# A seven-product QKV projection: row pairs 6 to 29 taken two at a time, all bf16 products of both first, then the float32r ones

## The chip, the cores and the metric

The kernel runs on one core of one Trainium2 chip. The metric is the device time of one execution in microseconds (us), as the median of several runs. The engines are named as the profile names them: PE (TensorE, matmuls), PEld (TensorE's weight loads), DVE (VectorE), ACT (ScalarE), POOL (GpSimd) and SP (SyncE, which here only issues DMAs).

## The reference

```python
# x: (16, 512, 768) float32, w_qkv: (768, 2304) float32
qkv = np.matmul(x, w_qkv)
q, k, v = qkv[..., :768], qkv[..., 768:1536], qkv[..., 1536:]
return np.stack([q, k, v], axis=0).astype(np.float32)
```

So 8192 rows of 768 are multiplied by a 768 x 2304 matrix, and the 2304 columns are stored as three outputs.

## The kernel before

**Tiling.** The 8192 rows are 32 *pairs* p of 2 x 128 rows. The 2304 columns are two *quads* q of 1024 columns each (0 to 1023, 1280 to 2303) and a *remainder* of 256 columns between them. Within a pair and a quad the product is a 2 x 2 block product: two row blocks of 128, two halves of the inner 768 (384 each, `KH` = 3 steps of 128), two column blocks of 512. It is done with seven block products instead of eight, from sums of the blocks of x and sums of the blocks of w. Each block product is three matmuls of 128 x 128 by 128 x 512 (`product`, L244). Products 1 and 2 use bf16 copies of x (`xb`) and w (`b1`). Products 3 to 7 use float32r sums of x (`s`, from `sums_x`) and of w (`t`, and the block `b22`). The remainder is a plain product in bf16: twelve matmuls of 256 columns per pair (`rem_row`, L299).

**A quad's work** is in `do(u, n)`. Three PSUM banks are used: x holds product 1 and then, added up in place, 6, 7 and 4; z holds product 2; y holds 5 and then 3. Each intermediate value of bank x is copied out by ACT (L253 after product 1, L269 after 6, L275 after 7, L279 after 4) into the output tile `o`, before the next product is added to the bank. DVE adds bank z to the first copy (L266), bank y to the copy after 7 (L276), and bank y again, once product 3 is in it, to the copy after 6 (L282). The eight PSUM banks come from one pool, and a new bank is one that its last reader has freed.

**A pair's x** goes through four steps. `load_x` brings it from HBM in four DMAs of 192 KB to `xin` (three buffers). `transpose` turns it on DVE (L154) into `xf` (two buffers). `round_x` casts it to bf16 on POOL (L191) into `xb` (four buffers). `sums_x` makes five float32r blocks on POOL (L211 to L215) in `s` (two buffers).

**Order.** The order is written by hand: the program order of each engine is the order of the calls. For pairs 3 to 30, `two(a, b, early)` issues for quads a and b of one pair: product 1 of both, the next pair's transpose, cast and sums (`ahead(p + 1)`) and the load of pair p + 2, the remainder, product 2 of both, then the ten float32r products 6, 6, 5, 7, 5, 7, 4, 3, 4, 3, with `store_quad` after each quad's product 3. A store of a quad is one DMA of 768 KB and one of 256 KB on SP's queue. Of a pair's four loads, two are issued on SP and two on ACT from pair 7 on. Pairs 0 to 2 are a start-up stage of their own, in which the weights are loaded, cast and summed; `last` does pair 31. The output tiles `o` have five buffers. One more tile, `both` (one buffer), serves the start-up and then holds one quad of pair 2.

Of the kernel before, what the change touches and what calls it, by code (L numbers as in the profile page):

```python
# [10 lines left out]
def kernel(  # L11
# [20 lines left out]
    nc = tc.nc  # L32
    P = 128
    G = 32
# [7 lines left out]
    NP = M // (2 * P)  # L42
# [18 lines left out]
    bt_pool = ctx.enter_context(tc.tile_pool(name="bt", bufs=1))  # L61
# [22 lines left out]
    both = bt_pool.tile([P, 2, KH * CB], fp32, name="both", tag="both")  # L84
# [37 lines left out]
    xin, xf, xb, sr = {}, {}, {}, {}  # L122
# [3 lines left out]
    def load_x_half(p, h, eng):  # L126
        rows = x_flat[p * 2 * P:(p + 1) * 2 * P, :].rearrange("(g b) k -> b g k", b=G)
        for i in (2 * h, 2 * h + 1):
            eng.dma_start(xin[p][i * G:(i + 1) * G], rows[:, :, i * KC:(i + 1) * KC])
# [12 lines left out]
    def load_x(p, other):  # L142
        xin[p] = xin_pool.tile([P, 2 * P // G, KC], fp32, name="xin")
        load_x_half(p, 0, nc.sync)
        if other is not None:
            load_x_half(p, 1, other)

    def transpose(p, parts=1):
        t = xf_pool.tile([P, KT, 2 * P], fp32, name="xf")
        turned = t[:].rearrange("p j (g b) -> p g j b", b=G)  # L150
        rows = xin.pop(p)[:].rearrange("p g (a j) -> p g j a", a=G)
        n = 2 * P // G // parts
        for g in range(0, 2 * P // G, n):
            nc.vector.transpose(turned[:, g:g + n], rows[:, g:g + n])  # L154
        xf[p] = t

# [27 lines left out]
            [xb[p][:, n, r * P:(r + 1) * P] for n in ks], [t[:] for t in ps]  # L186
        )

    def round_x(p):
        xb[p] = xb_pool.tile([P, KT, 2 * P], bf16, name="xb", tag="xb")  # L190
        nc.gpsimd.tensor_copy(out=xb[p][:], in_=xf[p][:])  # L191

    act, dve = nc.scalar, nc.vector

# [9 lines left out]
    def sums_x(p, eng=None):  # L204
        t = xf.pop(p)
        a11, a12 = t[:, :KH, :P], t[:, KH:, :P]
        a21, a22 = t[:, :KH, P:], t[:, KH:, P:]
        s = s_pool.tile([P, 5, KH, P], f32r, name="s")
        sr[p] = s
        sums = {  # L210
            1: lambda g: g.tensor_tensor(s[:, 1], a21, a22, op=add),  # L211
            2: lambda g: g.tensor_tensor(s[:, 2], s[:, 1], a11, op=sub),  # L212
            3: lambda g: g.tensor_tensor(s[:, 3], a11, a21, op=sub),  # L213
            0: lambda g: g.tensor_copy(out=s[:, 0], in_=a22),
            4: lambda g: g.tensor_tensor(s[:, 4], a12, s[:, 2], op=sub),  # L215
        }
        if eng is not None:
            return sums
        for n in (1, 2, 3, 0, 4):
            sums[n](nc.gpsimd)  # L220
# [5 lines left out]
    def quad(p, q, pool=o_pool, tag="o"):  # L226
        u = Quad()
        u.p, u.q = p, q
        u.o = pool.tile([P, 2, 2 * CB], fp32, name="o", tag=tag)
        u.x = u.y = u.z = None  # L230
        return u

    def product(u, n, ps, start):
        t1, t2, t3, t4 = ts[u.q]
        if n <= 2:
            h = (n - 1) * KH
            lhs = [xb[u.p][:, h + j, :P] for j in range(KH)]
            rhs = [b1[u.q][:, h + j, :] for j in range(KH)]
        else:
            k, t = {3: (4, b22[u.q][:]), 4: (0, t4), 5: (1, t1), 6: (2, t2), 7: (3, t3)}[n]  # L240
            lhs = [sr[u.p][:, k, j, :] for j in range(KH)]
            rhs = [t[:, j, :] for j in range(KH)]
        for j in range(KH):
            nc.tensor.matmul(  # L244
                ps[:], lhs[j], rhs[j],
                start=(start and j == 0), stop=(j == KH - 1), skip_group_check=True,
            )

    def bank():
        return ps_pool.tile([P, CB], fp32, name="ps")  # L250

    def evacuate(u):
        nc.scalar.activation(u.o[:, 0, :CB], u.x[:], ident)  # L253

    def do(u, n, out=True):
        c11, c12 = u.o[:, 0, :CB], u.o[:, 0, CB:]
        c21, c22 = u.o[:, 1, :CB], u.o[:, 1, CB:]
        if n == 1:
            u.x = bank()
            product(u, 1, u.x, True)  # L260
            if out:
                evacuate(u)
        elif n == 2:
            u.z = bank()
            product(u, 2, u.z, True)
            nc.vector.tensor_tensor(c11, c11, u.z[:], op=add)  # L266
        elif n == 6:
            product(u, 6, u.x, False)
            nc.scalar.activation(c12, u.x[:], ident)  # L269
        elif n == 5:  # L270
            u.y = bank()
            product(u, 5, u.y, True)
        elif n == 7:
            product(u, 7, u.x, False)
            nc.scalar.activation(c22, u.x[:], ident)  # L275
            nc.vector.tensor_tensor(c22, c22, u.y[:], op=add)  # L276
        elif n == 4:
            product(u, 4, u.x, False)
            nc.scalar.activation(c21, u.x[:], ident)  # L279
        elif n == 3:  # L280
            product(u, 3, u.y, False)
            nc.vector.tensor_tensor(c12, c12, u.y[:], op=add)  # L282
# [14 lines left out]
    def rem_row(p, r, ps):  # L297
        for j in range(KT):
            nc.tensor.matmul(  # L299
                ps, xb[p][:, j, r * P:(r + 1) * P], w_rem[j // KH][:, j % KH, :],  # L300
                start=(j == 0), stop=(j == KT - 1), skip_group_check=True,
            )

    def rem(p, eng=nc.sync, between=None):
        ps = ps_pool.tile([P, 2, REM], fp32, name="ps")
        rem_row(p, 0, ps[:, 0, :])
        if between is not None:
            between()
        rem_row(p, 1, ps[:, 1, :])
        return rem_copied(p, ps, eng)  # L310

    def rem_copied(p, ps, eng=nc.sync):

        def copied():
            o = or_pool.tile([P, 2, REM], fp32, name="orem")
            act.activation(o[:], ps[:], ident)  # L316
            return lambda: eng.dma_start(rows_of(1, p, R_OFF - H, R_OFF - H + REM), o[:])

        return copied
# [11 lines left out]
                        )  # L331
        return [rem_copied(p, ps) for p, ps in zip(pairs, banks)]

    def two(a, b, early, u=None):

        do(a, 1)
        do(b, 1, u is None)
        if u is None:
            early()
            rem(a.p)()()  # L340
        else:
            middle(u)
            copied = rem(a.p, between=lambda: third(u))
            evacuate(b)
            early()
            copied()()
            fourth(u)
        do(a, 2)
        do(b, 2)
        do(a, 6)  # L350
        do(b, 6)
        do(a, 5)
        do(a, 7)
        do(b, 5)
        do(b, 7)
        do(a, 4)
        do(a, 3)
        store_quad(a)
        do(b, 4)
        do(b, 3)  # L360
        store_quad(b)
# [14 lines left out]
    def last(a, b):  # L376

        p = a.p

        def rem_stored(r):  # L380
            ps = bank()
            rem_row(p, r, ps[:, :REM])
            o = or_pool.tile([P, 2, REM], fp32, name="orem")
            nc.scalar.activation(o[:, 0, :], ps[:, :REM], ident)  # L384
            row = (2 * p + r) * P
            nc.scalar.dma_start(out_flat[1, row:row + P, R_OFF - H:R_OFF - H + REM], o[:, 0, :])

        do(a, 1)
        do(b, 1)
        do(a, 2)  # L390
        do(a, 6)
        do(b, 2)
        do(b, 6)
        for u in (a, b):
            store_cols(u, 0, 0, CB, nc.sync)
        for u in (a, b):
            do(u, 5)
            do(u, 7)
            store_cols(u, 1, CB, 2 * CB, nc.sync)
        do(a, 4)  # L400
        store_cols(a, 1, 0, CB, nc.scalar)
        rem_stored(0)
        do(b, 4)
        store_cols(b, 1, 0, CB, nc.scalar)
        for u in (a, b):
            do(u, 3)
            store_cols(u, 0, CB, 2 * CB, nc.sync)
        rem_stored(1)


    ND = 2
# [21 lines left out]
    for h in range(2):  # L433
        rows = w_qkv.rearrange("(p j) n -> p j n", j=KT)[:, h * KH:(h + 1) * KH]
# [17 lines left out]
    quads = {}  # L452
# [45 lines left out]
    def fourth(u):  # L498
        do(u, 4)
        store_quad(u)  # L500

    def ahead(p):
        transpose(p)
        round_x(p)
        sums_x(p)
# [7 lines left out]
    turned = [turn_row(0, 0)]  # L513
# [49 lines left out]
    sums = sums_x(2, dve)  # L563
# [7 lines left out]
    u = quad(2, 0)  # L571
# [42 lines left out]
    u2 = quad(2, 1, bt_pool, "both")  # L614
    do(u2, 1)
    do(u2, 2)

    for p in range(ND + 1, NP):
        def early():
            if p + 1 < NP:  # L620
                ahead(p + 1)
            if p + 2 < NP:
                load_x(p + 2, nc.sync if p <= ND + 2 else nc.scalar)

        a, b = quad(p, 0), quad(p, 1)
        if p == ND + 1:
            two(a, b, early, u2)
        elif p < NP - 1:
            two(a, b, early)
        else:  # L630
            last(a, b)


# [28 lines left out]
```

## Time and profile before

| What | Value |
|---|---|
| Time, median of 3 runs | 360.9 us (360.07 to 361.46) |
| The profiled execution's own time | 360.84 us |
| Its span, first to last instruction | 359.1 us |
| Granted clock of TensorE, mean | 0.999 of full speed |
| PE busy | 353.6 us, 98% of the span |
| PEld, DVE, ACT, POOL busy | 70%, 64%, 52%, 50% |
| DMA: bytes, mean rate | 107.73 MB, 300 GB/s |

A group line of the profile gives the kernel's line, engine, operation, out<-in by the program's names, shapes, the count, then the busy time and the mean length in ns, and last the idle time of the engine ahead of these instructions with what ended it. Matmuls are pipelined, and their ends are modelled: the time that a matmul costs is the distance between starts, not its length. In the chain of waits and in a timeline, the first number is the start in us from the start of the span and the second is the length.

### The profile page before, as it was taken

What the parts mean: (1) busy time and instruction counts of PE and PEld (TensorE: products, weight loads), DVE (VectorE), ACT (ScalarE), POOL (GpSimd) and SP (SyncE); (2) the same over time, 40 slices, a digit from 0 to 9 for tenths busy, and PEclk for the clock granted to TensorE, in tenths of its full rate; (3) what the DMA queues carried; (4) which work ended last, traced back from release to release, by engine and by line L of the source; (5) the groups of instructions that cost most, each with busy time, mean ns of one, the idle gap of its engine ahead of it and who ended that gap; (6) DMA issues with size and microseconds to landing.
All of it is one profiled execution on the core that took longest, in us unless ns stands there. A gap on an engine that the chain in (4) does not pass through costs nothing.

```text
span 359.1 us, 5279 instructions
## 1 busy us (share of the span) xinstructions
PE 353.6 (98%) x1780; PEld 251.4 (70%) x1780; DVE 228.8 (64%) x244; ACT 185.7 (52%) x316; POOL 179.8 (50%) x187
## 2 busy tenths in 40 slices
PE   8999999999999999999999999999999999999995
PEld 3465577777777777777777777777777777777764
DVE  3789776666566675556676556676556676556643
ACT  5479644445444445444445444445544445545443
POOL 0223766446665445665444665444665444666420
PEclk9999999999999999999999999999999999999999
DMA  7998999898999998999999999898999899989767
GB/s 270 344 373 306 330 354 397 249 347 297 282 307 309 294 288 260 309 298 314 293 291 277 291 293 324 286 289 278 295 285 331 284 297 271 297 279 324 289 241 257
DMA packets 82106, 107.73 MB, mean 300 GB/s; under 512 B 5408, under 2 KB 62240, under 8 KB 82080
## 3 DMA queue, kind: packets, MB, share of 16 engines
q1 hardware_dynamic: 66672, 96.35, 82.1%
q10 hardware_dynamic: 14608, 10.65, 9.0%
q0 software_dynamic: 800, 0.39, 0.8%
q8 instruction: 14, 0.23, 0.3%
q14 instruction: 12, 0.10, 0.1%
HBM read 32.28 MB, written 75.50 MB: 300 GB/s over the span
## 4 chain that ended last, share of the span: by engine, by line
PE 92%; DMA 4%; ACT 2%; ACTq 1%; issue 0%
PE ps L244 78%; PE ps L299 10%; PE ps L472 4%; DMA st<-in_w_qkv_dram 3%; DMA touch<-in_x_dram 1%; PE ps L327 1%; ACT o L279 0%; ACTq L370 0%; ACT orem L316 0%; ACT o L462 0%; ACT orem L384 0%; ACT xb L200 0%; ACT both L448 0%; ACT o L253 0%; ACTq L416 0%
## 5 line engine op out<-in xcount | busy, mean ns | idle before, releaser
L244 PE MATMUL ps<-t,s 128*128 128x512 f32 x720 | 181.2, 399 | 0.1
L244 PEld LDWEIGHTS ps<-t,s 128*128 128x128 f32 x720 | 135.0, 188 | 31.1 <-ACT o L253 0.4
L191 POOL CAST xb<-xf 128x1536 bf16<-128x1536 f32 x28 | 40.9, 1462 | 131.4 <-DVE xf L154 131.4
L276 DVE TENSOR_TENSOR o<-o,ps 128x512 f32<-128x512 f32 x58 | 39.9, 688 | 90.7 <-ACT o L275 90.7
L154 DVE STREAM_TRANSPOSE xf<-xin 128x1536 f32<-128x1536 f32 (+1 forms) x32 | 88.9, 2782 | 2.3 <-DMA xin<-in_x_dram 2.3
L244 PE MATMUL ps<-b,xb 128*128 128x512 bf16 x360 | 87.7, 380 | 0.0
L244 PEld LDWEIGHTS <-xb 128*128 128x128 bf16 x360 | 32.8, 98 | 37.3 <-issue 7.6
L269 ACT ACTIVATE o<-ps 128x512 f32<-128x512 f32 x60 | 35.9, 598 | 43.8 <-PE ps L244 41.1
L275 ACT ACTIVATE o<-ps 128x512 f32<-128x512 f32 x58 | 34.7, 598 | 44.3 <-PE ps L244 44.3
L282 DVE TENSOR_TENSOR o<-o,ps 128x512 f32<-128x512 f32 x60 | 41.3, 688 | 21.4 <-PE ps L244 20.2
L244 PE MATMUL ps<-b,s 128*128 128x512 f32 x180 | 50.4, 389 | 0.0
L279 ACT ACTIVATE o<-ps 128x512 f32<-128x512 f32 x60 | 35.9, 598 | 24.5 <-PE ps L244 21.6
L253 ACT ACTIVATE o<-ps 128x512 f32<-128x512 f32 x60 | 35.8, 597 | 24.4 <-DVE o L282 20.6
L299 PE MATMUL ps<-w_rem,xb 128*128 128x256 bf16 x360 | 44.6, 273 | 0.0
L299 PEld LDWEIGHTS <-xb 128*128 128x128 bf16 x360 | 34.9, 98 | 11.1 <-issue 0.8
L266 DVE TENSOR_TENSOR o<-o,ps 128x512 f32<-128x512 f32 x60 | 37.8, 672 | 2.0 <-ACT o L253 1.3
L244 PEld LDWEIGHTS ps<-b,s 128*128 128x128 f32 x180 | 33.8, 188 | 7.1
L211 POOL TENSOR_TENSOR s<-xf 128x384 fp32r<-128x384 f32 x29 | 30.8, 1063 | 0.0
L212 POOL TENSOR_TENSOR s<-s,xf 128x384 fp32r<-128x384 f32 x29 | 29.4, 1013 | 2.3
L215 POOL TENSOR_TENSOR s<-xf,s 128x384 fp32r<-128x384 f32 x29 | 29.6, 1019 | 0.0
L213 POOL TENSOR_TENSOR s<-xf 128x384 fp32r<-128x384 f32 x29 | 29.4, 1015 | 0.0
L316 ACT ACTIVATE orem<-ps 128x512 f32<-128x512 f32 x31 | 18.5, 597 | 20.4 <-PE ps L299 19.9
(47 smaller groups left out, 127.0 us busy)
## 6 DMA issues: line engine op xcount, KB each, us to landing
out_dram<-o SPq DMA_DIRECT2D x62, 768.0 KB, 5.6
out_dram<-o SPq DMA_DIRECT2D x65, 256.0 KB, 4.2
xin<-in_x_dram SPq DMA_DIRECT2D x62, 192.0 KB, 6.9
xin<-in_x_dram ACTq DMA_DIRECT2D x50, 192.0 KB, 4.3
out_dram<-orem SPq DMA_DIRECT2D x31, 256.0 KB, 5.9
st<-in_w_qkv_dram SPq DMA_DIRECT2D x11, 256.0 KB, 5.1
st<-in_w_qkv_dram SPq DMA_DIRECT2D x3, 768.0 KB, 10.1
xin<-in_x_dram SPq DMA_DIRECT2D x4, 384.0 KB, 4.5
```

Of the source, the lines that this page charges most:

```text
L154: nc.vector.transpose(turned[:, g:g + n], rows[:, g:g + n])
L191: nc.gpsimd.tensor_copy(out=xb[p][:], in_=xf[p][:])
L211: 1: lambda g: g.tensor_tensor(s[:, 1], a21, a22, op=add),
L244: nc.tensor.matmul(ps[:], lhs[j], rhs[j], start=(start and j == 0), stop=(j == KH - 1), skip_group_check=True,)
L253: nc.scalar.activation(u.o[:, 0, :CB], u.x[:], ident)
L266: nc.vector.tensor_tensor(c11, c11, u.z[:], op=add)
L269: nc.scalar.activation(c12, u.x[:], ident)
L275: nc.scalar.activation(c22, u.x[:], ident)
L276: nc.vector.tensor_tensor(c22, c22, u.y[:], op=add)
L279: nc.scalar.activation(c21, u.x[:], ident)
L282: nc.vector.tensor_tensor(c12, c12, u.y[:], op=add)
L299: nc.tensor.matmul(ps, xb[p][:, j, r * P:(r + 1) * P], w_rem[j // KH][:, j % KH, :], start=(j == 0), stop=(j == KT - 1), skip_group_check= ...
```

## The change

Pairs 6 to 29 are done in groups of two by a new function `group(p)`. In a group PE does the bf16 work of both pairs (products 1 and 2 of the four quads, and both remainders), and then the float32r products of the first pair and of the second (`rounded`, split off from `two`). The first quad of a group takes the tile `both`.

POOL's order in a group is: the first sum of pair p + 1, the cast of pair p + 1, its other four sums, the cast of pair p + 2, and, once the first pair's float32r products are done, the sums of pair p + 2. DVE transposes pair p + 2 at the start of the group and pair p + 3 after the four product-2 adds.

Loads of x are all issued on SP: pairs p + 4 and p + 5 within the group. Before, pair p issues the load of pair p + 2; now pair 3 issues those of pairs 5 and 6, pair 4 that of pair 7, and pair 5 those of pairs 8 and 9. Pair 7's transpose is done in two halves within pair 5's float32r products. Pairs 30 and 31 are done singly, by `two` and `last`.

```diff
--- before.py
+++ after.py
@@ -145,14 +145,20 @@
         if other is not None:
             load_x_half(p, 1, other)
 
-    def transpose(p, parts=1):
+    def transpose(p, parts=1, split=False):
         t = xf_pool.tile([P, KT, 2 * P], fp32, name="xf")
         turned = t[:].rearrange("p j (g b) -> p g j b", b=G)
         rows = xin.pop(p)[:].rearrange("p g (a j) -> p g j a", a=G)
         n = 2 * P // G // parts
-        for g in range(0, 2 * P // G, n):
-            nc.vector.transpose(turned[:, g:g + n], rows[:, g:g + n])
+        turns = [
+            lambda g=g: nc.vector.transpose(turned[:, g:g + n], rows[:, g:g + n])
+            for g in range(0, 2 * P // G, n)
+        ]
         xf[p] = t
+        if split:
+            return turns
+        for turn in turns:
+            turn()
 
 
 
@@ -186,9 +192,10 @@
             [xb[p][:, n, r * P:(r + 1) * P] for n in ks], [t[:] for t in ps]
         )
 
-    def round_x(p):
+    def round_x(p, t=None):
+        t = xf[p] if t is None else t
         xb[p] = xb_pool.tile([P, KT, 2 * P], bf16, name="xb", tag="xb")
-        nc.gpsimd.tensor_copy(out=xb[p][:], in_=xf[p][:])
+        nc.gpsimd.tensor_copy(out=xb[p][:], in_=t[:])
 
     act, dve = nc.scalar, nc.vector
 
@@ -331,7 +338,7 @@
                         )
         return [rem_copied(p, ps) for p, ps in zip(pairs, banks)]
 
-    def two(a, b, early, u=None):
+    def two(a, b, early, u=None, turns=()):
 
         do(a, 1)
         do(b, 1, u is None)
@@ -347,12 +354,20 @@
             fourth(u)
         do(a, 2)
         do(b, 2)
+        rounded(a, b, turns)
+
+    def rounded(a, b, turns=()):
+
+        for t in turns[:1]:
+            t()
         do(a, 6)
         do(b, 6)
         do(a, 5)
         do(a, 7)
         do(b, 5)
         do(b, 7)
+        for t in turns[1:]:
+            t()
         do(a, 4)
         do(a, 3)
         store_quad(a)
@@ -615,20 +630,55 @@
     do(u2, 1)
     do(u2, 2)
 
-    for p in range(ND + 1, NP):
+    def group(p):
+
+        quads = [quad(p, 0, bt_pool, "both"), quad(p, 1)]
+        do(quads[0], 1)
+        do(quads[1], 1)
+        turned = xf[p + 1]
+        sums = sums_x(p + 1, nc.gpsimd)
+        sums[1](nc.gpsimd)
+        round_x(p + 1, turned)
+        for n in (2, 3, 0, 4):
+            sums[n](nc.gpsimd)
+        transpose(p + 2)
+        round_x(p + 2)
+        if p + 4 < NP:
+            load_x(p + 4, nc.sync)
+        rem(p)()()
+        do(quads[0], 2)
+        do(quads[1], 2)
+        quads += [quad(p + 1, q) for q in range(2)]
+        do(quads[2], 1)
+        do(quads[3], 1)
+        if p + 5 < NP:
+            load_x(p + 5, nc.sync)
+        rem(p + 1)()()
+        do(quads[2], 2)
+        do(quads[3], 2)
+        if p + 2 < NE:
+            transpose(p + 3)
+        rounded(*quads[:2])
+        sums_x(p + 2)
+        rounded(*quads[2:])
+
+    NG, NE = ND + 4, NP - 2
+    extra = {NG - 3: (NG, ), NG - 1: (NG + 3, )}
+    for p in range(ND + 1, NG):
+        late_turns = []
+
         def early():
-            if p + 1 < NP:
-                ahead(p + 1)
-            if p + 2 < NP:
-                load_x(p + 2, nc.sync if p <= ND + 2 else nc.scalar)
-
-        a, b = quad(p, 0), quad(p, 1)
-        if p == ND + 1:
-            two(a, b, early, u2)
-        elif p < NP - 1:
-            two(a, b, early)
-        else:
-            last(a, b)
+            ahead(p + 1)
+            for n in (p + 2 + (p > NG - 3), ) + extra.get(p, ()):
+                load_x(n, nc.sync)
+            if p == NG - 1:
+                late_turns.extend(transpose(NG + 1, 2, True))
+
+        two(quad(p, 0), quad(p, 1), early, u2 if p == ND + 1 else None, late_turns)
+    for p in range(NG, NE, 2):
+        group(p)
+    two(quad(NE, 0), quad(NE, 1), lambda: ahead(NE + 1))
+    last(quad(NE + 1, 0), quad(NE + 1, 1))
 
 
 # ---- launch: one core; inputs and outputs as the reference has them ----
```

## Prediction

> **What bounds the kernel now.** I read the page first (busy shares, groups), then the chain of waits in order of time, then TensorE's own timeline over one pair.
>
> ```profile
> span 359.1 us, 5279 instructions
> PE 353.6 (98%) x1780; PEld 251.4 (70%) x1780; DVE 228.8 (64%) x244; ACT 185.7 (52%) x316; POOL 179.8 (50%) x187
> PE 92%; DMA 4%; ACT 2%; ACTq 1%; issue 0%
> ```
>
> TensorE (PE) is on the chain for 92% of the span. The chain in order of time shows that from pair 4 on it never leaves PE:
>
> ```profile
> 195.39 1.31 PE ps L299 x12
> 196.70 9.43 PE ps L244 x42
> 206.13 1.31 PE ps L299 x12
> ```
>
> One pair is 206.13 - 195.39 = 10.74 us. An edit of the order can gain only by closing PE's own seams, and lose only by making PE wait. The seams are in PE's timeline (start, length, tile, count; ends are modelled, so starts are what to subtract):
>
> ```profile
> 181.14 0.84 PE L244 MATMUL ps<-b,s 128*128 128x512 f32 x3
> ...
> 183.18 1.47 PE L244 MATMUL ps<-b,xb 128*128 128x512 bf16 x6
> 184.49 1.47 PE L299 MATMUL ps<-w_rem,xb 128*128 128x256 bf16 x12
> 185.80 1.46 PE L244 MATMUL ps<-b,xb 128*128 128x512 bf16 x6
> 186.91 5.14 PE L244 MATMUL ps<-t,s 128*128 128x512 f32 x21
> 191.88 0.84 PE L244 MATMUL ps<-b,s 128*128 128x512 f32 x3
> ```
>
> Nine float32r products run from 181.14 to 183.18: 0.2267 us each. The twelve 256-wide ones take 1.31 us, 0.109 each. The sixth bf16 product of the last group is recorded at 186.88, so five steps take 1.08 us, 0.216 each. A pair without seams would be 30 x 0.2267 + 12 x 0.216 + 12 x 0.109 = 10.70 us. The seams cost 10.74 - 10.70 = 0.04 us per pair: about 0.015 where float32r gives way to bf16 (1.31 us for six, not 1.296), the rest at the start of the float32r run (21 products from 186.88 + 0.216 to 191.88 take 4.78 us, not 4.76). In that stretch GpSimd is casting:
>
> ```profile
> 187.00 1.46 POOL L191 CAST xb<-xf 128x1536 bf16<-128x1536 f32 x1 [4.78 <-DVE xf L154]
> ```
>
> **The change, part by part.**
>
> *Seams.* Pairs 6 to 29 are 24 pairs with 24 bf16 stretches now and 12 after. 12 x 0.04 = 0.48 us gained.
>
> *Casts out of the float32r run.* Each remaining seam loses its cast neighbour. The excess inside the float32r start is 0.02 us, so this is worth 0 to 0.02 us; I take 0.01 because the same stretch also holds the switch itself: 12 x 0.01 = 0.12 us. [...]
>
> *Matmul work.* The same 1780 matmuls; 0.
>
> *VectorE.* In a group, with T the start of its bf16 part (7.81 us) and F = T + 7.81 the start of the float32r part, the transpose of pair p+2 stands first and that of p+3 after the four bf16 adds. Durations and offsets come from VectorE's timeline (its pair's bf16 part starts at 193.92, its float32r part at 197.84):
>
> ```profile
> 194.12 0.69 DVE L282 TENSOR_TENSOR o<-o,ps 128x512 f32<-128x512 f32 x1 [0.67 <-PE ps L244]
> 194.72 2.94 DVE L154 STREAM_TRANSPOSE xf<-xin 128x1536 f32<-128x1536 f32 x1
> 197.59 1.25 DVE L266 TENSOR_TENSOR o<-o,ps 128x512 f32<-128x512 f32 x2
> 201.41 0.69 DVE L276 TENSOR_TENSOR o<-o,ps 128x512 f32<-128x512 f32 x1 [2.58 <-ACT o L275]
> ```
>
> First transpose: T + 0.8 to T + 3.75; then the adds of the first two product-2 banks end at T + 4.3 and T + 5.0. The bank of the first is taken again by the third quad's product 2 at T + 6.5: 2.2 us to spare. Second transpose: the fourth add starts 0.42 us after its last matmul (T + 7.59), ends at T + 8.7; the transpose runs T + 8.6 to T + 11.56. Queued behind it is the c22 add of the first quad (L276 now), free at F + 3.57 = T + 11.4, so 0.1 us late: T + 11.5 to T + 12.17. Waiting for that is product 3 into the same bank, the eighth float32r product, due at F + 21 x 0.2267 = T + 12.57, its weight load at T + 12.35. That leaves some 0.1 us after the semaphore. Cost 0, cover thin.
>
> *GpSimd.* It may overwrite the sums' buffer 0.2 us after T, then runs 1.01 + 1.46 (cast p+1) + 1.01 + 1.01 + 0.50 + 1.02 + 1.46 (cast p+2): ends at T + 7.7, inside the bf16 part. Pair p+1's cast is needed at T + 3.9 and there at T + 2.7; its sums at T + 14.6 and there at T + 6.2. Cost 0.
>
> *Stores and buffers.* The first quad of a group uses the single "both" buffer: stored at T + 14.2, wanted again at T + 22.5 (8.3 us), and ScalarE can be late by some 4 us before the bank above is late. Stores of 768 KB land in 5.6 us by the page's median; the longest landing of any transfer in 95 to 200 us is 7.9. Cost 0.
>
> *Loads of x.* All go to SP's queue, behind stores; ScalarE issues none. In groups they are issued some 20 us before their transpose; now it is about 10. The risk is only where grouping starts: pairs 6 to 8 are loaded one pair earlier than now and pair 9 two, in the busiest stretch. There VectorE already waits for x:
>
> ```profile
> 66.32 2.97 DVE L154 STREAM_TRANSPOSE xf<-xin 128x1536 f32<-128x1536 f32 x1 [0.39 <-DMA xin<-in_x_dram]
> ...
> 77.38 2.97 DVE L154 STREAM_TRANSPOSE xf<-xin 128x1536 f32<-128x1536 f32 x1 [0.71 <-DMA xin<-in_x_dram]
> ```
>
> Four 192 KB loads take 2.4 us of the engines (ScalarE's queue: 9.0% of 359.1 us for 10.65 MB). Pair 8's loads take the place of pair 7's with one pair's loads more ahead: 77.38 + 2.4. Against that, SP now stands 3.8 us behind a load that ScalarE issued, and the windows show the engines idle for it:
>
> ```profile
> 60.00:65.00 5.00, 5.00 (x23) 3.96 (x22) 2.06 (x3) 2.63 (x5) 4.05 (x5) 1.00 1.06 328
> 65.00:70.00 5.00, 5.00 (x30) 3.34 (x30) 4.37 (x4) 2.11 (x5) 0.58 (x1) 1.00 0.95 311
> 70.00:75.00 5.00, 5.00 (x24) 4.13 (x23) 2.21 (x4) 2.83 (x5) 4.92 (x6) 1.00 0.72 222
> ```
>
> A DMA share of 0.72 (next to last column) is 1.4 us unused, which the extra loads fill: 77.38 + 2.4 - 1.4 = 78.4. The transpose ends at 81.35, the add behind it at 81.95; group 6 starts at T = 75.78 and wants the bank at 82.28. It just fits: 0, with a bound of 1.1 us if the 1.4 us cannot be used and 2.5 us if SP's FIFO costs as much again. The split transpose of pair 7 pushes two adds of pair 5 back by up to 1.6 us, to 77.3, where nobody waits yet.
>
> *Ends.* Start-up to pair 3 and pairs 30 and 31 keep their order: 0.
>
> **Sum.** 360.84 (the profiled execution: 359.1 span plus 1.7 around it) - 0.48 - 0.12 = 360.2. The profiled execution is 0.06 us below the median of the three runs shown, so I forecast 360.3 us, no change that counts. 0.5% is 1.8 us, about what a measurement of this kernel can tell from no change; its runs spread over 1.4 us.
>
> **The rivals.**
>
> *A, slower: the x of pair 8 comes too late.* For it: the two waits above, and DMA shares over 1.0 up to 65 us. Against: the idle 1.4 us, and that the stall happens once, because in groups x has 20 us. It decides once pair 8's transpose starts after 78.8; each us later is one us. To lose 1.8 us net it must start after 81.1. Price 0.5 to 3 us: 360.8 to 363.3.
>
> *B, slower: the second transpose holds the c22 add in every group.* For it: only 0.1 us of cover. Against: the transpose's length hardly varies (2.94 to 2.97 in steady pairs). If the add is 0.2 us later than I have it, PE waits 0.1 us in each of 11 groups: 1.1 us, 361.4; to pass 0.5% it must be 0.3 us later.
>
> *C, faster by over 0.5%.* All seams of 24 pairs are 24 x 0.04 = 1.0 us; even with every one gone it is 359.9. This needs something that the trace doesn't show, 359.0 or less.
>
> *D: the change doesn't do what it says*, since PE was already dense: 360.9 with no gain. This too is "no change".
>
> **Chances.** Forecast and D together, with the small stalls of A and B: 0.76. A beyond 0.5%: 0.11; B beyond it: 0.08. C: 0.05. The range reaches down to 359.5 (all seams gone, and the runs' scatter) and up to 362.6 (A at 2.4 us, or B at 0.2 us per group).
>
> **What would show it.** Right: PE's period per group falls from 21.48 to about 21.43 us; 12 bf16 stretches of 7.8 us; GpSimd's casts inside them; no wait of PE for VectorE. A wrong: a PE gap of over 0.5 us near 82 us, released by VectorE's product-2 add behind a transpose that waited for x. B wrong: a gap before the eighth float32r product of every group, released by the c22 add. If ScalarE's first copy of a group waits for a store by 4 us or more, the buffer count was misjudged.

## The result

The changed kernel takes 361.72 us (median of 14 runs, 361.23 to 362.92), the kernel before, run beside it, 360.79 (14 runs, 360.07 to 361.54): a ratio of 1.0026, 95% interval 1.0018 to 1.0034. So it is slower by 0.9 us, where the prediction's sum had 0.6 us of gain, and the loss is well outside the scatter of the medians though still within 0.5%. The profiled execution of the changed kernel is 362.42 us with a span of 360.6, and so 0.7 us above its own median.

The page of the changed kernel (the lines that answer to those of before), and then its chain of waits over one group:

```profile
span 360.6 us, 5230 instructions
PE 353.2 (98%) x1780; PEld 252.0 (70%) x1780; DVE 230.5 (64%) x245; ACT 186.0 (52%) x316; POOL 177.0 (49%) x187
...
PE 91%; DMA 6%; ACT 1%; ACTq 1%; DVE 0%; issue 0%; DVEq 0%
```

```profile
121.14 1.31 PE ps L306 x12
122.45 2.59 PE ps L251 x12
125.04 1.31 PE ps L306 x12
126.36 16.23 PE ps L251 x72
142.58 1.31 PE ps L306 x12
```

A group of two pairs is one remainder, twelve bf16 matmuls, the other remainder and 72 others: 142.58 - 121.14 = 21.44 us. Two pairs were 21.48 before, 21.43 was forecast. TensorE stays on the chain through the whole steady part. What was lost is elsewhere, and a table of stretches shows where. All times are starts of TensorE's remainders: that of pair 4 (the last ahead of the grouping is pair 5's), of pair 30, and the second one of pair 31, which is the last remainder.

| Profile | Pair 4 at | Pair 4 to 30 | Pair 30 to last remainder | Last remainder to end | Span |
|---|---|---|---|---|---|
| before | 55.61 | 279.24 | 19.59 | 4.63 | 359.07 |
| after | 56.62 | 278.80 | 19.59 | 5.63 | 360.64 |

Three differences: the start 1.01 us later, the groups 0.44 us shorter, and the last stretch 1.00 us longer. The start's instructions are issued in the same order in both kernels; the first loads of x and w landed later (the third load of x at 7.36 us, not 6.80). The last stretch was "0" in the prediction. The chain of waits there, before:

```profile
354.83 0.44 ACTq L370
355.27 0.04 issue
355.31 0.02 ACTq L384
```

and after:

```profile
355.39 0.44 ACTq L385
355.83 0.32 issue
356.15 0.02 ACTq L399
```

ACTq is ScalarE's sequencer, and "issue" is time in which the engine waits for nothing that the profile shows. Between the DMA that it has issued and the wait ahead of its last copy, ScalarE stands still for 0.32 us instead of 0.04. SP does the same at its very end: its drain (L707), an instruction of the program's end, starts 0.34 us after the last wait is over, not 0.04. The view of the DMA queues from 350 to 361 us holds a line that before does not have there:

```profile
q14 instruction: 3, 0.02, 0.6%
```

The page calls q14's packets instructions: over the whole span 0.11 MB in 14 packets, 8 KB each. The trace does not say which engine a packet is for. Counting each engine's instructions in the trace from 0, the same kind of pause stands ahead of places 191, 319 and 447 of ScalarE, and 79, 207, 335 and 463 of SP, as far as each kernel reaches them: every 128 instructions, 0.32 to 0.43 us instead of 0.04. (Ahead of ScalarE's 63, and of its 191 after the change, it can't be seen, because the engine waits for something else there.) Such a place is called a block start here, and the 128 instructions from one to the next a block. In the last stretch a packet of q14 starts after each of the two: 1.32 us after ScalarE's (356.15 and 357.47) and 0.64 us after SP's (359.68 and 360.32). The pause is over by then, so this packet isn't what the engine waited for. What it brings, and what the pause itself waits for, is not shown. The third packet, at 351.37, belongs to neither place. After the change, ScalarE issues no more loads of x and has 455 instructions instead of 529; SP issues them all and has 468 instead of 405. That put ScalarE's 447 and SP's 463 into the last 6 us. Before the change both engines had passed their last block start by 304.31 us.

**Theory T:** where an engine passes a block start at the end of the kernel, it costs time there, and this is what the change lost; which places they are depends only on how many instructions each engine has. **Rival S:** the loss is the later start, a property of the change. **Rival Q:** it is SP's fuller queue, or the grouping. **Rival N:** scatter.

### The profile page after: what moved, and what is told of

Same layout as the page of the kernel before. It is cut to its first block, busy times and chain, and to the rows that moved or that the text cites. A ratio compares the mean times of both kernels' runs of the same rounds, so it can differ in the third digit from the quotient of the medians.

```text
span 360.6 us, 5230 instructions
## 1 busy us (share of the span) xinstructions
PE 353.2 (98%) x1780; PEld 252.0 (70%) x1780; DVE 230.5 (64%) x245; ACT 186.0 (52%) x316; POOL 177.0 (49%) x187
## 4 chain that ended last, share of the span: by engine, by line
PE 91%; DMA 6%; ACT 1%; ACTq 1%; DVE 0%; issue 0%; DVEq 0%
PE ps L251 78%; PE ps L306 10%; DMA st<-in_w_qkv_dram 3%; PE ps L487 3%; DMA xin<-in_x_dram 1%; DMA touch<-in_x_dram 1%; DVE xf L154 0%; ACT o L286 0%; ACTq L385 0%; ACT xb L207 0%; ACT orem L399 0%; ACT o L260 0%; ACT orem L323 0%; ACTq L431 0%; ACTq L401 0%
## 5 line engine op out<-in xcount | busy, mean ns | idle before, releaser
L251 PE MATMUL ps<-t,s 128*128 128x512 f32 x720 | 178.6, 396 | 0.1
L154 DVE STREAM_TRANSPOSE xf<-xin 128x1536 f32<-128x1536 f32 (+1 forms) x33 | 91.1, 2764 | 1.7 <-DMA xin<-in_x_dram 1.6
L251 PE MATMUL ps<-b,xb 128*128 128x512 bf16 x360 | 85.6, 380 | 0.0
L283 DVE TENSOR_TENSOR o<-o,ps 128x512 f32<-128x512 f32 x58 | 39.7, 684 | 60.7 <-ACT o L282 60.7
L251 PEld LDWEIGHTS <-xb 128*128 128x128 bf16 x360 | 33.7, 98 | 37.0 <-issue 4.7
L276 ACT ACTIVATE o<-ps 128x512 f32<-128x512 f32 x60 | 36.0, 599 | 36.4 <-PE ps L251 33.9
L306 PEld LDWEIGHTS <-xb 128*128 128x128 bf16 x360 | 34.8, 98 | 11.3 <-issue 1.1
```

What stands on the lines that cost most here:

```text
L154: lambda g=g: nc.vector.transpose(turned[:, g:g + n], rows[:, g:g + n])
L251: nc.tensor.matmul(ps[:], lhs[j], rhs[j], start=(start and j == 0), stop=(j == KH - 1), skip_group_check=True,)
L306: nc.tensor.matmul(ps, xb[p][:, j, r * P:(r + 1) * P], w_rem[j // KH][:, j % KH, :], start=(j == 0), stop=(j == KT - 1), skip_group_check= ...
```

## The experiments

### The same two kernels again

> The changed kernel again, for a second profile. Its first profile is 1.01 us behind the profile of before by pair 4, gains 0.44 us from pair 4 to pair 31, and loses 0.95 us more after TensorE's last matmul. Theory T (instruction blocks): ScalarE's instruction 447 (counted from 0 in the trace; its earlier block starts are 63, 191, 319) and SP's 463 (earlier 79, 207, 335) fall into the last 6 us, where each must wait for its block to be fetched; so the tail is the same as in the first profile: from the last remainder's start to the end of the span 5.5 to 5.7 us (before: 4.6), with 8 KB instruction fetches near 357 and 360. Rival S (start-up): the 1.0 us at the start is a property of the change; then it comes back, 0.8 to 1.2 us. Rival N (run-to-run scatter): both differ, the start by any amount and the tail back near 4.6 us. T with scatter at the start only: time 361.4 to 362.0, tail the same, start anywhere from 0 to 1 us.

> The kernel before once more, for the scatter: ratio 1.000 with its interval, and a second profile. Rival S: pair 4's remainder starts at 55.7 to 55.9 as in the first profile of before. Rival N: it starts anywhere from 55.5 to 57. Tail under theory T: 4.6 us from the last remainder's start to the end, with no instruction fetch in it.

Measured: the change 361.81 us (6 runs, ratio 1.0030, 1.0018 to 1.0041), the kernel before 360.98 (11 runs, ratio 1.0002, 0.9993 to 1.0011).

| Profile | Pair 4 at | Pair 4 to 30 | Pair 30 to last remainder | Last remainder to end | Span |
|---|---|---|---|---|---|
| change again | 55.65 | 279.02 | 19.59 | 5.62 | 359.88 |
| before again | 55.86 | 279.24 | 19.59 | 4.64 | 359.33 |

The start's 1.0 us is gone: scatter of the start, rival S falls. The last stretch is the same to 0.01 us, for both kernels, with packets of q14 at 356.72 and 359.57 in the change: rival N falls. That each engine waits there for a block to be fetched, as the expectation has it, is not shown: here too ScalarE's pause is over at 355.40, 1.32 us ahead of the first of these packets. The second profile alone adds up: 0.04 (start) - 0.22 (groups) + 0.99 (end) = 0.81, which is 359.88 - 359.07. And the groups gained only half of the first profile's 0.44; that is taken up below.

### Moving the block starts out of the end

First ScalarE's alone, by two one-column copies more in each group, ahead of its copy after product 6, where it stands idle (1.38 us in the change's timeline, L276 at 192.71; the 4 us of the expectation are not shown):

```diff
         if p + 2 < NE:
             transpose(p + 3)
+        for _ in range(2):
+            act.activation(tiny[:], tiny[:], ident)
         rounded(*quads[:2])
```

> The change, with two one-column ScalarE copies more in each of the 12 groups, ahead of the float32r products, where ScalarE waits some 4 us for product 6 anyway. ScalarE then starts its block at instruction 447 some 24 instructions earlier, ahead of the last pair; SP's place 463 stays in the tail. Theory T: the wait of 0.3 us before ScalarE's last copy goes, and if the fetch's packet was what made the last store land 0.57 us later, that goes too; SP's 0.34 us at the drain stays: 0.3 to 0.7 us faster than the change, 361.0 to 361.4. Rivals S and N, and any that looks for the loss in loads, stores or grouping: the same as the change within 0.15 us, or slower by up to 0.2 for the extra work.

Measured: 361.17 us (11 runs), 0.64 below the change on the same chip, with 24 instructions more. The last stretch is 5.07 us (5.62), and ScalarE's pause is back to normal:

```profile
355.08 0.44 ACTq L385
355.52 0.04 issue
355.57 0.02 ACTq L399
```

SP's stays. A view of its instructions of the last line (minimum, median and maximum in ns) still has the drain that takes 131 ns, after a pause of 0.34 us:

```profile
L709 SPq EVENT_SEMAPHORE  x8: 17/28/28, 356.5 to 359.7; - x8
L709 SPq DRAIN  x3: 7/7/131, 358.8 to 359.2; - x3
```

Then both, by giving half of the load of pair p + 4 back to ScalarE's queue in the first 8 groups:

```diff
         if p + 4 < NP:
-            load_x(p + 4, nc.sync)
+            load_x(p + 4, nc.scalar if p < NG + 16 else nc.sync)
```

> The change, with half of the load of pair p+4 (two of its four transfers) given back to ScalarE's queue in the first 8 groups: 16 instructions fewer on SP, which then ends before its place 463, and 19 more on ScalarE, whose 447 falls ahead of the last pair. Theory T: neither block start lies in the tail; from the last remainder's start to the end of the span 4.5 to 4.8 us as before the change; 0.7 to 1.0 us faster than the change, 360.7 to 361.0, with the gain of 0.44 us in the groups kept; if the start is no later than before, 360.2 to 360.5. Rival S or a loss in the grouping: the same as the change, 361.5 to 361.9. Rival Q (SP's queue carries too much): also faster, but then spread over the groups and not in the tail.

Measured: 360.80 us (11 runs, ratio 0.9998, 0.9989 to 1.0007), 1.01 below the change. The last stretch is 4.65 us, as before the change. SP's drain:

```profile
L707 SPq DRAIN  x3: 7/7/7, 358.2 to 358.5; - x3
```

The gain lies in the last stretch and not spread over the groups, so rival Q falls too: pairs 4 to 30 take 279.00 us, 0.02 less than in the change. For SP's part there is no edit that moves its block start and leaves its queue alone: this one also takes 16 loads from the queue. SP's part rests on the pause itself, which is 0.34 us ahead of the drain in the three profiles in which place 463 falls there, and 0.04 in the ten others.

ScalarE's block start has not vanished: it now lies ahead of its second copy after product 1 of pair 31, where the copy is 0.3 us late and TensorE loses 0.07 us.

### The same loss made in the kernel before

If T holds, the kernel before must lose the same without any grouping, once it has the right number of instructions. In `two`, ahead of product 6:

```diff
         do(a, 2)
         do(b, 2)
+        for _ in range(2 + (a.p >= 10)):
+            act.activation(tiny[:], tiny[:], ident)
         do(a, 6)
```

> The kernel before, with two or three one-column ScalarE copies more in each of pairs 3 to 30, ahead of product 6, where ScalarE waits for TensorE; the number is such that ScalarE's next block start, 575, falls on the wait ahead of its very last copy, where 447 fell in the change. Nothing is grouped, no load is moved. Theory T: 0.3 us of waiting at that place, an 8 KB fetch near 357 us, the last 512 KB-side store landing 0.5 us later: 0.4 to 0.7 us slower than the kernel before, 361.3 to 361.6. Any rival that blames the grouping or the loads: no change, 360.8 to 361.1.

> The control: the kernel before with 43 such copies (one in each of pairs 3 to 15, two in each of 16 to 30). ScalarE ends some 24 instructions short of block start 575. Theory T: as the kernel before, 360.8 to 361.1, no fetch in the last 10 us. If the tiny copies themselves cost: about half of what the other kernel with 77 of them loses.

Measured: with 77 copies 361.89 us (ratio 1.0025, 1.0015 to 1.0034), last stretch 5.19 us; with 43 copies 361.44 (1.0010, 1.0000 to 1.0020), last stretch 4.63. The direction is T's, but the control was not at 0. The control's profile lay 0.83 us late at pair 4, all of it by the 20th microsecond, with unchanged pairs after that. Three more runs on one chip, with another control that has still more copies (`3 + (a.p >= 10)`, 105 in all), so that the block start lies ahead of the last pair, at 338.43 us:

> The kernel before with still more tiny copies on ScalarE, three or four in each of pairs 3 to 30 (105 in all), so that its block start 575 lies 36 instructions before its end, ahead of the last pair's copies and no longer in the last 6 us. Theory T: although it does more work than the kernel with 77 copies, it is 0.5 to 0.6 us faster than that one, its tail from the last remainder's start to the end 4.6 us instead of 5.2. If the copies themselves cost (0.42 with 43, 0.87 with 77 so far, about 0.01 us each): 1.0 to 1.2 us slower than the kernel before, slower than with 77.

> The control with 43 copies again: it was 0.42 us above the kernel before, and its profile lay 0.8 us late by the 20th microsecond, ahead of all that was changed, with the same steady pairs and the same tail. If that was scatter of the start: 0 to 0.2 us above the kernel before. If the start depends on the program: 0.3 to 0.5 again, and late by the 20th microsecond again.

> The kernel with 77 copies again, on the same chip as its two controls. Theory T: 0.45 to 0.65 us above the one with 105 and above the one with 43, tail 5.2 us.

| Kernel | Time | Ratio to before | Last stretch | Pair 4 at | Pair 4 to 30 |
|---|---|---|---|---|---|
| 43 copies | 361.12 | 1.0010 (1.0001 to 1.0020) | 4.64 | 55.52 | 279.24 |
| 77 copies, block start at the end | 361.95 | 1.0029 (1.0018 to 1.0040) | 5.20 | 56.43 | 279.24 |
| 105 copies | 361.23 | 1.0012 (1.0002 to 1.0021) | 4.64 | 56.49 | 279.24 |

The kernel with 105 copies is 0.72 us faster than the one with 77. So it is not the copies, it is where the block start lies. With 77, the chain has the pause of the change, and with 105 it has not:

```profile
355.66 0.44 ACTq L372
356.10 0.32 issue
356.42 0.02 ACTq L386
```

```profile
355.72 0.44 ACTq L372
356.16 0.04 issue
356.20 0.02 ACTq L386
```

The expectation of 0 for the controls failed: in their three runs they are 0.2 to 0.4 us above the kernel before. In the two control profiles that are late, all of it lies ahead of the 20th microsecond, before any copy is issued; in the third there is no delay at all. Over all thirteen profiles of this study, pair 4 starts anywhere from 55.45 to 56.62 us. Why these kernels start late more often is open.

### What thinned the gain in the groups

In the second profile of the change the group takes 21.467 us, not 21.44. The distances between the starts of TensorE's matmuls show one place: products of a float32r run come every 227 ns, but from the first matmul of the eighth product on they are 232, 236, 228, 233 and 231 ns, in 10 of the 11 groups after which another group follows. In the last group they are 227: it alone has no second transpose ahead of the c22 add. (In the first profile of the change it was 2 groups of 11; in the runs with 24 copies and with 8 loads moved, 10 and 9.) VectorE's timeline in one of these groups, whose float32r run starts at 190.75:

```profile
191.80 3.09 DVE L154 STREAM_TRANSPOSE xf<-xin 128x1536 f32<-128x1536 f32 x1
194.79 0.67 DVE L283 TENSOR_TENSOR o<-o,ps 128x512 f32<-128x512 f32 x1
```

The c22 add (L283) has no idle time ahead of it: it is held by the transpose, and ends at 195.46. PEld's timeline has the weight load of the eighth product right behind it:

```profile
195.51 0.64 PEld L251 LDWEIGHTS ps<-b,s 128*128 128x128 f32 x3
```

Where nothing holds this load, it starts 4.750 us after the start of the run (the last group; every group of the test below); here it starts 4.763 after. So the load is 13 ns late, and with the matmuls' way back to their pace the group is 26 ns longer. In the first profile of the change the same transposes take 3.07 to 3.08 us, the add ends 4.68 to 4.70 us after the start of the run instead of 4.71, and only two groups lose anything, 20 ns each. This is the prediction's rival B, at 26 ns a group. The test splits the second transpose, with the means that `rounded` has for pair 7, and moves the block starts well away from the end:

```diff
-            load_x(p + 4, nc.sync)
+            load_x(p + 4, nc.scalar if p < NG + 20 else nc.sync)
...
-        if p + 2 < NE:
-            transpose(p + 3)
-        rounded(*quads[:2])
+        turns = transpose(p + 3, 2, True) if p + 2 < NE else ()
+        rounded(*quads[:2], turns)
```

> The change with half of the load of pair p+4 on ScalarE's queue in the first 10 groups (no block start of ScalarE or SP in the last 10 us) and the second transpose of a group in two halves, the second behind both c22 adds. Theory B' (the thin cover of the prediction's rival B is used up by a hair: in the new profiles TensorE loses 25 ns at the eighth float32r product of 9 or 10 groups, and none in the last group, which has no second transpose): the 25 ns go, the group's period falls from 21.465 to 21.44 us, 0.2 to 0.3 us in all; 360.4 to 360.7, ratio to the kernel before 0.9985 to 0.9995. Rival (the 25 ns are the clock or the products' own): the period stays 21.465 and the time 360.8 to 360.9.

Measured: 360.47 us (12 runs, 360.06 to 360.94) beside 361.02 for the kernel before: ratio 0.9981, 0.9971 to 0.9991. Every group takes 21.44 us, pairs 4 to 30 take 278.76, the last stretch 4.64. The add now waits for ScalarE's copy and not for the transpose:

```profile
191.50 1.63 DVE L154 STREAM_TRANSPOSE xf<-xin 128x768 f32<-128x768 f32 x1
194.21 0.69 DVE L283 TENSOR_TENSOR o<-o,ps 128x512 f32<-128x512 f32 x1 [1.08 <-ACT o L282]
```

This version beats both kernels: the gain of the grouping is real, 0.5 us, and the change as it was made gave it back twice.

### Rival A, once

In the profile with the 24 copies, one group is 0.63 us longer than the others. VectorE's timeline at its start, and the chain:

```profile
79.78 2.97 DVE L154 STREAM_TRANSPOSE xf<-xin 128x1536 f32<-128x1536 f32 x1 [2.66 <-DMA xin<-in_x_dram]
```

```profile
82.31 0.66 PE ps L251 x3
82.97 0.03 DVEq L273
83.01 0.33 DVE o L273
83.33 0.04 issue
83.38 15.80 PE ps L251 x69
```

The transpose of pair 8 waited 2.66 us for x, the product-2 add behind it was late, and the fourth quad's product 2 waited for its bank: rival A, one product later than foretold (the third quad's, of which the prediction spoke, had run just ahead of it without a wait). To see whether it matters, the grouping was started two pairs later (`NG, NE = ND + 6, NP - 2`, loads on ScalarE's queue for `p < NG + 18`):

> As the kernel with moved blocks and the split transpose, but the grouping starts at pair 8, two pairs later (11 groups), so that the loads ahead of it are issued after the crowded stretch up to 80 us. In one of the new profiles (24 tiny copies) TensorE lost 0.63 us once near 82 us behind a transpose that waited 2.66 us for x: the prediction's rival A. Theory A' (that stall comes in a part of the executions): the median falls by 0.1 to 0.4 us and the spread of the runs shrinks, against one seam more (0.04): 360.1 to 360.5. Rival (the stall is rare): the same as with grouping from 6, within 0.1, 360.4 to 360.7.

Measured: 360.65 us (12 runs, 360.15 to 361.61; ratio 0.9987, 0.9975 to 0.9999), no better than 360.47, and not with a smaller spread. The stall is there in one of the five profiles of kernels that group from pair 6; as a cost of the median it is not shown.

## Why the prediction was wrong, step by step

**Ends, 0: this step failed.** It argued from the order of the calls: the same order at the end, so the same time. But the change moved 50 DMA instructions from ScalarE to SP, and with them the places at which these engines pass from one block of 128 instructions to the next. The term measures +0.99 us (5.62 against 4.63). Its parts can be taken from the last stretch: ScalarE's block start alone +0.56 (5.20 against 4.64 with the copies), SP's alone +0.43 (5.07 against 4.64), together 0.99. ScalarE's part is the 0.26 to 0.28 us by which its last store is issued late, and 0.28 to 0.30 us of longer landing: 2.65 to 2.68 us from issue to landing in the four profiles with the block start at ScalarE's last copy, 2.37 to 2.39 in the nine others. The last packet of that store starts 2.24 us after the issue in the second profile of the change (355.87 to 358.11) and 2.02 in the one with 8 loads moved (355.75 to 357.77). In the late case the last eight 1 KB packets run one after the other when all others are done (42 to 43 ns apart, from 358.52 to 358.82 in the first profile of the change). That fits one DMA engine that had the 8 KB of instructions to carry (q14's packet starts at 356.72 there, within this store); the trace does not name the engine, so the reason for the longer landing is argued, not shown. SP's part is the pause of 0.34 us, not 0.04, and the drain of 130 ns, not 7.

In the steady part these pauses cost TensorE nothing: in the kernel before, ScalarE's end at 132.45, 218.24 and 304.31 us, SP's at 177.55 and 303.23, and the pairs there take 10.74 us like the others. At the end they cost time: ScalarE's pause is 0.32 us on the chain and SP's, ahead of its drain, 0.34, each 128 instructions after the engine's place before, with packets of 8 KB on q14.

**Seams, 0.48: the mechanism was right.** Pairs 4 to 30 gained 0.48 us where nothing else stood in the way (279.24 to 278.76, the version with the split transpose), and 0.44 in the first profile of the change, where two groups lost 0.02 each.

**Casts, 0.12: this step failed too.** The prediction puts half of an excess of 0.02 us a seam down to the cast. In the traces of before and after, the cast beside TensorE's matmuls cost nothing. After the change GpSimd does nothing at the start of the float32r run; its timeline has the last cast end at 191.40, ahead of the run, which starts at 191.64, and then 7.5 us of idle time:

```profile
189.93 1.47 POOL L198 CAST xb<-xf 128x1536 bf16<-128x1536 f32 x1
198.90 1.02 POOL L218 TENSOR_TENSOR s<-xf 128x384 fp32r<-128x384 f32 x1 [7.50 <-PE ps L251]
```

The excess stayed all the same. The mean distances from the second to the third float32r matmul of a run, and so on to the eighth (starts, runs between 70 and 335 us), were 224.1, 230.6, 235.8, 228.2, 232.4 and 230.7 ns before, with the cast beside them, and 224.0, 231.0, 236.0, 228.0, 232.9 and 230.6 after, without: 22 ns over 6 x 226.7 both times. So it comes with the switch from bf16 to float32r, and belongs to the seam that it was counted with.

**VectorE, 0 with thin cover: mis-sized.** The due time was right: the prediction has the eighth product's weight load at T + 12.35, and in the second profile an unhindered one starts at T + 12.37 (T, the start of the bf16 part, is 183.13 in the group shown). What was mis-sized is the c22 add, which ends at T + 12.33 and not T + 12.17: the transpose starts at T + 8.67, not 8.6, and takes 3.09 us, not 2.96. (Why it takes longer there than the kernel before's 2.94 to 2.96 is not shown.) So all of the cover was used, and the weight load was late by 13 ns. Rival B's mechanism occurs, but each group costs 0.026 us, not 0.1: 0.26 us over ten groups, less than a tenth of a per cent and not the half that was feared.

**Loads, 0: right, on an estimate that was too late.** Pair 8's transpose was forecast for 78.4 with group 6 at T = 75.78, 2.6 us behind the group's start. It started only 1.6 us behind it: at 78.39 with the group at 76.80 in the first profile of the change, without a wait, and at 77.48 with the group at 75.82 in the second, with a wait of 0.17 us. So x was there a microsecond earlier than the sum has it, and that 78.39 looks like the forecast is luck: that profile started 1.0 us late. Rival A came true in one profile, where the transpose started 4.15 us behind the group's start. By the prediction's price (one us for each us past 78.8) that costs 1.1 us. It cost 0.63; the product that waited was due 0.65 us later than the one that the prediction names.

**Matmul work, GpSimd, stores and buffers, 0: right.** There are 1780 matmuls; GpSimd's work fits the bf16 part; no wait of TensorE for a store or a bank appears in the groups of the change's two profiles (the list of waits for 100 to 330 us has no line for PE).

**The sum.** From the second profile of the change: -0.22 for the groups (seams 0.48, less 0.26 from rival B) and +0.99 at the end is +0.77. The medians differ by 0.91 and 0.93; the rest is put down to the scatter of the start, which is not shown. The time still lies in the range that the prediction gives, 359.5 to 362.6, but only because that range is wide: its upper end was worked out for rivals A and B, and neither made this loss.

## What to carry to other kernels

In this kernel, moving 50 DMA instructions from ScalarE to SP also moved the places, 128 instructions apart, at which each engine pauses for 0.32 to 0.43 us. When a change moves DMAs or copies between engines, count each engine's instructions, find such places from the pauses in the trace that nothing explains ("issue" in the chain, instruction packets in the view of the DMA queues), and see that none falls into the last microseconds, where the two here cost 0.99 us; a few instructions moved to another queue, or added where an engine is idle, were enough here. And a cover of 0.1 us that is worked out from one timeline is no cover: where a wait lands that close, split the long instruction ahead of it in the same edit.

## What the runs showed of the hardware

- In the profiles of the kernel before and of the change, ScalarE and SP pause at every 128th instruction where it can be seen, for 0.32 to 0.43 us where 0.04 is usual; the packets of q14, which the page calls instructions, are 8 KB each. At the end of this kernel one such place cost 0.43 (SP) or 0.56 us (ScalarE); over pair 31's second copy it cost TensorE 0.07 us; in the middle of the kernel before, the pairs with ScalarE's places 191, 319 and 447 take 10.74 us like the others.
- A float32r run that begins behind bf16 matmuls takes until its eighth matmul to get to its pace of 226.7 ns, 22 ns in all, before and after; where its weight load was held for 13 ns, five distances of 228 to 236 ns followed, 26 ns in all, with much the same pattern.
- The start, which is the same in all these kernels, scatters by over 1 us from one execution to another (pair 4 at 55.45 to 56.62 us; 55.65 and 56.62 for the change alone), from the landing of the first loads on. A difference of 1 us between two single profiles is no result until the stretch that it lies in is seen twice.
